# Query up projection in packed tiles, one mean and one square sum per norm, and the norms' factors made on all partitions

## The chip, the core and the metric

The kernel runs on one core of a Trainium2 chip. The metric is the device time of one execution in microseconds (us), as the median of several runs. Times are told with the names of the core's engines: TensorE (PE, its weight loads PEld), VectorE (DVE), ScalarE (ACT), GpSimd (POOL) and SyncE (SP, which issues the DMAs).

## What is computed

One sequence of 512 tokens with 1024 channels goes through two blocks of two layers each; weights and activations are fp32. Cut to what the change touches:

```python
# first block, layer i = 0, 1
y = mixer_ab(x, ...) if i == 0 else mixer_c(x, ...)
x = layer_norm(ALPHA * x + y, ln_mix_g[i], ln_mix_b[i])
f = conv_ffn(x, ...)
x = layer_norm(ALPHA * x + f, ln_ffn_g[i], ln_ffn_b[i])
x = x + sigmoid(x @ ple_w_gate[i]) * (p[i] @ ple_w_proj[i])

# second block, layer l = 0, 1
h = rms_norm(x, norm_g[l])          # then four branches, gates, merge
x = x + acc @ w_out
# at the end
return rms_norm(x, final_norm_g)

# inside mixer_ab: eight heads, 64 channels without and 32 with a rope
cq = rms_norm(h[..., o3:o4], q_norm, RMS_EPS)             # 384 channels
qb = (cq @ w_q_up).reshape(B, S, 8, 64 + 32)
qb = concat([qb[..., :64], apply_rope(qb[..., 64:], cos_b, sin_b, 32)])
ckv = rms_norm(h[..., o4:o5], kv_norm, RMS_EPS)           # 256 channels
```

A layer norm subtracts the mean over the channels, divides by the root of the variance plus 1e-5, and applies a gain and a bias; an RMS norm divides by the root of the mean square plus 1e-6 and applies a gain.

## The kernel before

**Layout.** Activations lie with channels on the 128 partitions and the 512 tokens along the free dimension; x is eight such tiles (slots, named `s`). A weight matrix comes by DMA in 512 KB pieces (`st`), which ACT copies into a rounded high part `h` and DVE into the rest `l`; activations are split likewise. A product of two such operands is three fp32r matmuls (`mm3`: high by high, high by low, low by high). Sums lie in PSUM banks named by their tag: three `d`, two `S`, one `o`, two `m`. Ordinary fp32 operands, which the norms' matmuls have, take two records per matmul in the trace.

**Norms.** A norm over channels needs sums across partitions. Whole projections that end in a norm are done in halves of 256 tokens (`HALVES`); the norm of the first half runs while PE does the second half of the projection, and that of the second half while PE does the first half of what follows (`project`, `group`, `tick`). There are 4 layer norms (8 halves; `Layernorm`) and 3 RMS norms (6 halves; `Rms`: ahead of each layer of the second block, and at the very end), and the two whole-width norms of the latents in `mixer_ab` (`rms`). In a layer norm, `feed` adds up the tiles as they come, in two partial sums on POOL; three matmuls with the constant matrix `meanw` (1/1024 everywhere) sum both and the last tile into a bank, on all partitions. DVE subtracts the mean, ACT squares, DVE and POOL add the squares in two partial sums (`square`). `rstd` makes the factor: one matmul per 128 tokens and partial sum, with the squares as weights and one column of `meanw` moving, puts the sum of each token on a partition; DVE adds epsilon, POOL raises to -0.5; and a matmul with that column as weights, spread over 128, and the identity moving, puts the factor on all partitions again. DVE multiplies (out of PSUM), ACT applies gain and bias (layer norm) and copies the high part, DVE subtracts to get the low part, and PE's next products read both.

**Query up projection.** `prepb(j)` makes the queries of heads 2j and 2j+1: per head one tile of 96 output channels (64 and 32), nine matmuls with 96 weight columns each, a rope over all 96 rows (`rope`: two DVE instructions and two on POOL; the table has 1 and 0 for the first 64 rows), and a split (ACT, DVE).

**The order of the work.** The program is first recorded (`Rec.add`) and then put in order by a planner (`Rec.order`): each engine takes, of the operations that its estimates show as ready, the one with the lowest key; the key is the place in the recording, changed by the table `MOVES` (292 entries of the form first:count, engine, shift). The order of the recording in the first mixer is written out in `ORDER_AB`. All instructions are issued from one line, L680, so the profile shows that line for all of them and groups are told apart by tile names. Activation tables are placed when the program is built: a load stands ahead of a function that the set then loaded does not hold.

Of the kernel before, what the change touches and what calls it, by code (L numbers as in the profile page):

```python
# [13 lines left out]
F32R = mybir.dt.float32r  # L14
# [3 lines left out]
ALU = mybir.AluOpType  # L18
# [59 lines left out]
def _consts():  # L78
# [31 lines left out]
    for i in range(128):  # L110
        r = i % 64
        if r < 16:
            sel[8 + r % 8, 0, i] = 1
            sel[r % 8, 1, i] = -1 if r < 8 else 1
        else:
            sel[64, 0, i] = 1
        if i < 64:
            sel[64, 2, i] = 1
        else:
            r = i % 32  # L120
            sel[32 + r % 16, 2, i] = 1
            sel[16 + r % 16, 3, i] = -1 if r < 16 else 1
# [27 lines left out]
def _layout(i):  # L150
# [14 lines left out]
    a["qup"] = _tiles(i["ab_w_q_up"][0], 6, 96)  # L165
# [95 lines left out]
820:255v-105 1084:103*+49 722:36v-308 1616:34*+52 1965:4*+14 1574:51*+93 1106:7*+62 84:34*+626 1159:22*-127  # L261
446:33*-615 1906:60t-81 505:117*-42 787:69*-425 106:162*+401 1350:14t+359 402:130t-96 1746:61t+219 1011:260t+64
1380:106v+460 455:44*-78 485:18*+14 1162:31*+39 1176:17*-377 357:12*+199 1135:15*-23 878:153v+150 492:14t+120
96:144*-557 1108:293s-272 1022:243t+39 181:3t+644 0:113*+27 1743:5t+166 1168:15*+283 1353:360s-107 1071:22*+71
1904:22t-6 1516:181t+70 1939:14t+72 1100:6t+326 2125:8*-41 1399:10*-553 1807:4t-263 28:268*+13 2076:4*-686
1539:268*-30 1467:52v+164 1150:2*+99 1021:181*-30 1538:41t-149 1235:39v+248 1457:10*+20 1141:185*-5 1496:91*+12
1531:52*+9 1235:13*-270 1172:13t+230 1394:128*-30 1206:5*+87 1745:4*+494 1190:23*-5 2083:3s+246 1321:78t-26
1356:40*-12 1340:33t-505 1313:22*-111 1688:3*-272 1795:17*+172 1117:171*-15 1133:72*+5 1366:97*-9 2113:27t+652
1178:3t+63 1611:2*-399 1211:39v+291 1148:271*+20 1639:52*-116 1111:37*-182 1223:259v+350 1323:88*+59 953:325*+61
1436:33*-22 1137:38*-415 1103:155*-74 1105:7*+610 1474:13t-115 970:219t-128 1115:72*+45 796:392t-38 2073:70*+536  # L270
1077:2t-261 560:47*-252 1165:24t+37 617:6t-333 1668:27t-195 2123:5*+10 2081:210v-9 1181:34*-242 1467:2*-37
1122:21*-213 1138:255t+17 1106:70*+151 4567:114*-71 6914:44*-527 6986:17t-94 6524:388v+762 4439:113*-732 6522:9*-420
# [1940 lines left out]
```

## Time and profile before

| | before |
|---|---|
| median of 3 runs | 2402.99 us (2402.49 to 2403.5) |
| the profiled execution | 2402.8 us |
| its span in the trace | 2401.0 us |
| PE busy | 2378.2 us, 12100 matmul records |
| DVE, ACT, POOL busy | 1433.7, 1017.1, 489.7 us |
| mean granted clock of PE | 0.999 of full speed |
| table loads on ACT | 4 of 1283 ns |

Busy time is the union of an engine's instructions; matmuls overlap in it, so the time that one matmul adds is read from the chain of work that ended last, or from the starts of its neighbours, and not from its mean duration.

### The profile page before, as it was taken

How to read it: one execution, taken by the hardware profiler on the slowest of the kernel's cores; microseconds unless marked ns; L12 is line 12 of the kernel's file. 1: busy time of each engine (PE TensorE's matmuls, PEld its weight loads, DVE VectorE, ACT ScalarE, POOL GpSimd, SP SyncE). 2: the span in 40 equal slices, each digit the busy share in tenths (PEclk: the TensorE clock that was granted, in tenths of full speed). 3: DMA queues.
4: the chain of work that ended last, by engine and by line, in shares of the span. 5: the costliest groups of instructions: out<-in, count | busy, mean ns of one | idle time of the engine just before them, and what ended most of it. 6: DMA issues, size and time to landing. Idle time of an engine off the chain costs nothing.

```text
span 2401.0 us, 31174 instructions
## 1 busy us (share of the span) xinstructions
PE 2378.2 (99%) x12100; PEld 1927.6 (80%) x12100; DVE 1433.7 (60%) x2433; ACT 1017.1 (42%) x1732; POOL 489.7 (20%) x453
## 2 busy tenths in 40 slices
PE   9999999999999999999999999999999999999998
PEld 6766788888888777988888998777788987777887
DVE  5587775354475857664454765667643646686435
ACT  5564463242364646542332554433233334433232
POOL 1332321010131421220110330411222103111221
PEclk9999999999999999999999999999999999999999
DMA  5112222233233113232322252221323432213331
GB/s 191 54 35 73 77 91 97 97 97 97 88 113 100 55 52 97 79 115 97 97 97 97 80 172 88 80 75 49 113 98 117 143 99 78 79 45 104 106 96 62
DMA packets 73513, 220.87 MB, mean 92 GB/s; under 512 B 9557, under 2 KB 13397, under 8 KB 73366
## 3 DMA queue, kind: packets, MB, share of 16 engines
q1 hardware_dynamic: 73366, 218.89, 28.3%
q8 instruction: 95, 1.56, 0.3%
q14 instruction: 52, 0.43, 0.1%
HBM read 210.46 MB, written 8.39 MB: 91 GB/s over the span
## 4 chain that ended last, share of the span: by engine, by line
PE 95%; DVE 2%; ACT 2%; issue 1%; DMA 1%; SPq 0%; POOL 0%; POOLq 0%; DVEq 0%; ACTq 0%
PE d L680 76%; PE S L680 11%; PE m L680 4%; PE o L680 4%; ACT s L680 1%; DVE s L680 1%; DVE sm L680 0%; DVE l L680 0%; DMA s<-in_x 0%; DVE S L680 0%; DMA s<-in_pos 0%; ACT h L680 0%; SPq L680 0%; DVE mt L680 0%; POOL s L680 0%
## 5 line engine op out<-in xcount | busy, mean ns | idle before, releaser
L680 PE MATMUL d<-s,h 128*128 128x512 f32 (+1 forms) x5536 | 1659.8, 380 | 2.8 <-ACT s L680 1.8
L680 PEld LDWEIGHTS d<-s,h 128*128 128x128 f32 x5536 | 1013.7, 188 | 205.9 <-issue 17.5
L680 PE MATMUL d<-s,l 128*128 128x512 f32 (+1 forms) x2768 | 1040.2, 378 | 0.0
L680 DVE TENSOR_TENSOR l<-st,h 128x1024 fp32r<-128x1024 f32 (+3 forms) x379 | 467.0, 1236 | 511.5 <-ACT h L680 504.9
L680 ACT ACTIVATE h<-st 128x1024 fp32r<-128x1024 f32 (+4 forms) x379 | 388.5, 1026 | 815.9 <-PE d L680 656.9
L680 POOL TENSOR_TENSOR s<-s,s 128x512 f32<-128x512 f32 (+3 forms) x319 | 407.0, 1281 | 1118.4 <-DVE s L680 550.1
L680 PEld LDWEIGHTS d<-s,l 128*128 128x128 f32 x2768 | 520.1, 188 | 98.3 <-issue 5.3
L680 ACT ACTIVATE s<-s 128x512 f32<-128x512 f32 (+6 forms) x515 | 270.4, 542 | 356.7 <-DVE s L680 264.9
L680 DVE TENSOR_TENSOR s<-s,s 128x256 fp32r<-128x256 f32 (+6 forms) x337 | 198.7, 603 | 82.9 <-ACT s L680 68.8
L680 PE MATMUL S<-s,s 64*128 64x512 f32 (+10 forms) x752 | 173.0, 378 | 2.7 <-ACT s L680 2.1
L680 PEld LDWEIGHTS S<-s,s 64*128 64x128 f32 (+5 forms) x752 | 103.0, 185 | 63.4 <-ACT s L680 20.8
L680 POOL TENSOR_SCALAR s<-s 128x512 f32<-128x512 f32 x44 | 29.1, 662 | 570.9 <-ACT s L680 570.7
L680 PE MATMUL S<-s,h 128*128 128x256 f32 x704 | 143.5, 285 | 0.1
L680 DVE TENSOR_TENSOR s<-d,s 128x512 f32<-128x512 f32 (+4 forms) x135 | 79.6, 592 | 101.3 <-PE d L680 99.0
L680 DVE SCALAR_TENSOR_TENSOR s<-s,d 128x512 f32<-128x512 f32 x152 | 103.6, 682 | 32.8 <-PE d L680 30.4
L680 DVE SCALAR_TENSOR_TENSOR s<-s,s 128x512 f32<-128x512 f32 (+4 forms) x143 | 100.8, 708 | 37.2 <-ACT s L680 36.1
L680 PEld LDWEIGHTS S<-s,h 128*128 128x128 f32 x704 | 114.4, 191 | 1.3 <-issue 0.8
L680 PE MATMUL S<-s,l 128*128 128x256 f32 x352 | 99.4, 284 | 0.1
L680 ACT ACTIVATE s<-d 128x512 f32<-128x512 f32 (+3 forms) x159 | 89.2, 564 | 22.1 <-PE d L680 21.9
L680 PE MATMUL o<-s,s 128*128 128x128 f32 (+4 forms) x576 | 95.3, 407 | 0.0
L680 ACT ACTIVATE s<-S,sm 128x512 f32<-128x512 f32 x96 | 65.2, 683 | 61.8 <-DVE sm L680 61.8
L680 PE MATMUL d<-h,s 128*128 128x512 f32 (+1 forms) x252 | 79.4, 377 | 5.7 <-ACT s L680 5.7
(148 smaller groups left out, 1455.4 us busy)
## 6 DMA issues: line engine op xcount, KB each, us to landing
st<-in_win SPq DMA_DIRECT2D x112, 512.0 KB, 3.4
st<-in_gu SPq DMA_DIRECT2D x88, 512.0 KB, 3.4
st<-in_dn SPq DMA_DIRECT2D x44, 512.0 KB, 3.4
st<-in_pg SPq DMA_DIRECT2D x16, 512.0 KB, 3.4
st<-in_cqk SPq DMA_DIRECT2D x16, 512.0 KB, 3.4
st<-in_wbr SPq DMA_DIRECT2D x16, 512.0 KB, 3.5
st<-in_wo SPq DMA_DIRECT2D x16, 512.0 KB, 3.5
st<-in_abin SPq DMA_DIRECT2D x14, 512.0 KB, 3.2
```

Source lines behind the costliest of these rows:

```text
L680: getattr(getattr(s.nc, o.eng), o.call)(*[val(v) for v in o.args], **{k: val(v) for k, v in o.kw.items()})
```

## The change

Four edits to the computation, and a new table of moves.

1. The weight of the query up projection is laid out in six tiles of 128 columns instead of eight of 96: the 32 rope channels of four heads in one tile (two such tiles), the 64 other channels of two heads in one (four). `prepb` runs the rope on a tile of four heads once in two calls, splits it, and copies the parts into the heads' slots.
2. A layer norm's `feed` adds all eight tiles into one sum, the last two on DVE; one matmul makes the mean.
3. The two partial sums of squares are added on DVE before PE sums them.
4. `rstd` does one matmul with the constant matrix as weights and the sum of squares moving, 256 columns (512 in `rms`), which gives the mean square on all partitions; the factor is then made there: DVE adds epsilon, ACT does Ln and Exp with a scale of -0.5, and three DVE instructions refine the result (one Newton step). It lies in an SBUF slot, and the multiplications read it from there.
5. `MOVES` has 845 entries.

```diff
-    a["qup"] = _tiles(i["ab_w_q_up"][0], 6, 96)
+    wq = i["ab_w_q_up"][0].reshape(384, 8, 96)
+    rp, np_ = (lambda h: wq[:, h:h + 4, 64:].reshape(384, 128)), (lambda h: wq[:, h:h + 2, :64].reshape(384, 128))
+    a["qup"] = _tiles(np.concatenate([rp(0), np_(0), np_(2), rp(4), np_(4), np_(6)], 1), 6)
...
 MOVES = """
-820:255v-105 1084:103*+49 722:36v-308 1616:34*+52 1965:4*+14 1574:51*+93 1106:7*+62 84:34*+626 1159:22*-127
...
-    def rstd(s, ts, w, eps, c=slice(0, 512), tag="m", ticks=0):
+    def rstd(s, t, w, eps, c=slice(0, 512), tag="m", ticks=0):
         nc = s.nc
-        q0, n = c.start // 128, (c.stop - c.start) // 128
-        pm = s.bank(tag)
-        for q in range(q0, q0 + n):
-            for i, t in enumerate(ts):
-                nc.tensor.matmul(pm[:, q:q + 1], lhsT=t[:, 128 * q:128 * q + 128], rhs=w, start=i == 0,
-                                 stop=i == len(ts) - 1)
-        r = s.small(4)
-        nc.vector.tensor_scalar(r[:, :n], pm[:, q0:q0 + n], eps, None, op0=ALU.add)
-        s.pow_(r[:, :n], r[:, :n])
+        pm, r, u = s.bank(tag), s.slot(), s.slot()
+        p, q, v = pm[:, c], r[:, c], u[:, c]
+        nc.tensor.matmul(p, lhsT=w, rhs=t[:, c], start=True, stop=True)
         yield ticks
-        pb = s.bank(tag)
-        for q in range(n):
-            o = c.start + 128 * q
-            nc.tensor.matmul(pb[:, o:o + 128], lhsT=r[:, q:q + 1].to_broadcast([128, 128]), rhs=s.ident, start=True,
-                             stop=True)
-        return pb
+        nc.vector.tensor_scalar(v, p, eps, None, op0=ALU.add)
+        nc.scalar.activation(q, v, AF.Ln)
+        nc.scalar.activation(q, q, AF.Exp, scale=-0.5)
+        nc.vector.scalar_tensor_tensor(v, v, -0.5, q, op0=ALU.mult, op1=ALU.mult)
+        nc.vector.tensor_mul(v, v, q)
+        nc.vector.scalar_tensor_tensor(q, v, 1.5, q, op0=ALU.add, op1=ALU.mult)
+        s.free(u)
+        return r
...
+            nc.vector.tensor_add(ts[0][:, c], ts[0][:, c], ts[1][:, c])
+            pb = yield from s.rstd(ts[0], s.meanw, RMS_EPS, c, "mo"[i], 2)
...
-            if j % 4 == 0:
-                t[i, j // 4] = s.slot()
-            elif j % 4 == 1:
-                s.pool_add(t[i, j // 4][:, c], X[j - 1][:, c], X[j][:, c])
-            elif j != 7:
-                s.pool_add(t[i, j // 4][:, c], t[i, j // 4][:, c], X[j][:, c])
+            if j == 0:
+                t[i] = s.slot()
+            elif j == 1:
+                s.pool_add(t[i][:, c], X[0][:, c], X[1][:, c])
+            elif j < 6:
+                s.pool_add(t[i][:, c], t[i][:, c], X[j][:, c])
+            else:
+                s.nc.vector.tensor_add(t[i][:, c], t[i][:, c], X[j][:, c])
...
-            for k, t in enumerate((t0, t1, X[7])):
-                nc.tensor.matmul(pm[:, c], lhsT=s.meanw, rhs=t[:, c], start=k == 0, stop=k == 2)
+            nc.tensor.matmul(pm[:, c], lhsT=s.meanw, rhs=n.t[i][:, c], start=True, stop=True)
...
-            pb = yield from s.rstd(acc, s.meanw[:, :1], LN_EPS, c, tag, 2)
+            nc.vector.tensor_add(acc[0][:, c], acc[0][:, c], acc[1][:, c])
+            pb = yield from s.rstd(acc[0], s.meanw, LN_EPS, c, tag, 2)
...
-        s.meanq = mk("meanq", [128, 1], 1.0 / 384)
-        s.meank = mk("meank", [128, 1], 1.0 / 256)
+        s.meanq = mk("meanq", [128, 128], 1.0 / 384)
+        s.meank = mk("meank", [128, 128], 1.0 / 256)
...
+            if j % 2 == 0:
+                rq = s.rope(s.dense("qup", (0, 3)[j // 2], L["cq"]), CB, SB, ROT16)
+                L["rq"] = s.split(rq)
+                s.free(rq)
+            yield
+            pq = s.dense("qup", (1, 2, 4, 5)[j], L["cq"])
             for e in range(2):
-                rq = s.rope(s.dense("qup", 2 * j + e, L["cq"], m=96), CB, SB, ROT16, 96)
-                QB[j, e] = s.split(rq, 96)
-                s.free(rq)
-                yield
+                qh, ql = QB[j, e] = s.slot(F32R), s.slot(F32R)
+                r, o = slice(64 * e, 64 * e + 64), 32 * (2 * j % 4 + e)
+                nc.scalar.activation(qh[:64], pq[r], AF.Copy)
+                nc.vector.tensor_sub(ql[:64], pq[r], qh[:64])
+                nc.vector.tensor_copy(qh[64:96], L["rq"][0][o:o + 32])
+                nc.scalar.activation(ql[64:96], L["rq"][1][o:o + 32], AF.Copy)
```

How the instructions stand is read from the built programs. First ACT, in the second half of the layer norm behind the mixer of layer 1. Before, the squares (`s_8985`, `s_8992`) are followed by a weight copy (`h`), an evacuation (`s<-d`) and the gain and bias of the first tile:

```order
L680 ACTIVATE s_8985<-s_7911 128x256
L680 ACTIVATE s_8992<-s_7920 128x256
L680 ACTIVATE h_8997<-st_8759 128x1024
L680 ACTIVATE s_9009<-d_8874 128x512
L680 ACTIVATE s_7847<-s_7847,c_cols 128x256
L680 ACTIVATE s_8889<-s_7847 128x256
```

In the change, at the same place (`s_8978` is the factor; the first instruction on it is Ln, the second Exp):

```order
L744 ACTIVATE s_8937<-s_7849 128x256
L744 ACTIVATE s_8956<-d_8819 128x512
L744 ACT_TABLE_LOAD
L744 ACTIVATE s_8978<-s_8970 128x256
L744 ACT_TABLE_LOAD
L744 ACTIVATE s_8978<-s_8978 128x256
L744 ACTIVATE s_7794<-s_7794,c_cols 128x256
L744 ACTIVATE s_8757<-s_7794 128x256
```

Four instructions have come in, two of them loads of activation tables. The same pattern stands in 12 of the 14 halves; only the first layer norm has Ln and Exp without loads. The built program has 28 table loads where that of before has 4.

Then PE at the same norm. Before (`o_9007` takes the sums, `o_9039` is the broadcast):

```order
L680 MATMUL o_9007<-meanw,s_8843 128x1
L680 MATMUL d_8899<-s_8943,l_8826 128x256
L680 MATMUL o_9007<-meanw,s_8848 128x1
L680 MATMUL o_9007<-meanw,s_8843 128x1
L680 MATMUL o_9007<-meanw,s_8848 128x1
...
L680 MATMUL S_9031<-s_8915,h_8997 128x256
L680 MATMUL o_9039<-identr,sm_9021 128x128 x2
L680 MATMUL S_9031<-s_8925,h_8997 128x256
...
L680 MATMUL S_9031<-s_8981,l_9012 128x256
L680 MATMUL d_8895<-s_8889,h_8720 128x256
```

In the change (`o_8965` is the one product; `s_8757` is the first tile of the normalized half, which the last two rows read):

```order
L744 MATMUL S_8830<-s_8813,l_8788 128x256
L744 MATMUL o_8965<-s_8895,meanw 128x256
L744 MATMUL S_8830<-s_8826,h_8734 128x256
...
L744 MATMUL S_8885<-s_8837,h_8871 128x256
L744 MATMUL S_8885<-s_8861,h_8871 128x256
L744 MATMUL S_8885<-s_8837,l_8961 128x256
L744 MATMUL S_8885<-s_8757,h_8871 128x256
L744 MATMUL S_8830<-s_8757,h_8734 128x256
```

The four sums and two broadcasts are one product, and 28 products of 256 columns stand between it and the first that reads a normalized tile; before, 33 of them and the broadcast stand between the last sum and the first reader (`s_8889`).

## Rows read from the trace of the kernel before

**Rows 1.** The page: engines' busy time, and the chain's shares by engine.

```profile
PE 2378.2 (99%) x12100; PEld 1927.6 (80%) x12100; DVE 1433.7 (60%) x2433; ACT 1017.1 (42%) x1732; POOL 489.7 (20%) x453
...
PE 95%; DVE 2%; ACT 2%; issue 1%; DMA 1%; SPq 0%; POOL 0%; POOLq 0%; DVEq 0%; ACTq 0%
```

**Rows 2.** The chain in order of time (start us, us, engine and tile, count).

```profile
330.64 316.62 PE d L680 x1401
```

**Rows 3.** The chain from 676 to 705 us: its longest piece.

```profile
683.20 3.62 ACT s L680 x11
```

**Rows 4.** The chain at norms: latents, a mean, ordinary products, sums, a broadcast.

```profile
123.71 2.77 PE m L680 x24
...
130.49 0.89 PE m L680 x8
...
660.59 1.30 PE m L680 x6
661.88 1.42 PE d L680 x12
...
1894.17 0.79 PE m L680 x8
...
1897.93 0.44 PE m L680 x4
```

**Rows 5.** Groups by form: out<-in, shapes, count | busy us, mean ns | idle before.

```profile
L680 PE MATMUL d<-s,h 128*96 128x512 f32 x48 | 16.4, 408 | 0.5 <-DVE s L680 0.5
...
L680 PE MATMUL d<-s,l 128*96 128x512 f32 x24 | 9.6, 401 | 0.0
...
L680 PE MATMUL o<-meanw,s 128*128 128x1 f32 x56 | 7.4, 233 | 1.3 <-DVE s L680 1.3
...
L680 PE MATMUL m<-s,meanw 128*128 128x256 f32 x24 | 6.4, 387 | 0.0
...
L680 PE MATMUL o<-identr,sm 128*128 128x128 f32 x28 | 4.3, 277 | 1.0 <-POOL sm L680 1.0
```

**Rows 6.** Timeline of the end: start us, us, instruction [idle before <-releaser].

```profile
2391.18 0.42 DVE L680 TENSOR_TENSOR s<-s,s 128x256 f32<-128x256 f32 x1 [0.48 <-ACT s L680]
...
2391.66 0.83 PE L680 MATMUL o<-meanw,s 128*128 128x1 f32 x6 [1.31 <-DVE s L680]
...
2394.28 3.22 DVE L680 SCALAR_TENSOR_TENSOR s<-s,c_cols,o 128x256 f32<-128x256 f32 x8 [1.59 <-PE o L680]
```

**Rows 7.** Timeline of a layer norm's second half behind layer 1's mixer.

```profile
1003.14 0.72 PE L680 MATMUL o<-meanw,s 128*128 128x1 f32 x6
...
1005.72 0.60 PE L680 MATMUL o<-identr,sm 128*128 128x128 f32 x4
...
1006.36 1.74 DVE L680 TENSOR_TENSOR s<-s,o 128x256 f32<-128x256 f32 x5 [2.03 <-PE o L680]
...
1006.82 0.60 ACT L680 ACTIVATE s<-s,c_cols 128x256 f32<-128x256 f32 x1 [3.33 <-DVE s L680]
...
1007.46 0.42 ACT L680 ACTIVATE s<-s 128x256 fp32r<-128x256 f32 x1
...
1008.20 0.28 PE L680 MATMUL d<-s,h 128*128 128x256 f32 x1
```

**Rows 8.** Groups by form: DVE's three-operand instruction on 256 columns.

```profile
L680 DVE SCALAR_TENSOR_TENSOR s<-s,s 128x256 f32<-128x256 f32 x24 | 12.8, 551 | 4.3 <-ACT s L680 4.1
```

**Rows 9.** Timeline of ACT around two table loads.

```profile
18.09 1.06 ACT L680 ACTIVATE h<-st 128x1024 fp32r<-128x1024 f32 x1 [1.27 <-DMA st<-in_abv]
19.17 1.28 ACT L680 ACT_TABLE_LOAD   x1
24.51 0.63 ACT L680 ACTIVATE s<-s 64x512 f32<-64x512 f32 x1 [4.06 <-DVE s L680]
25.16 1.28 ACT L680 ACT_TABLE_LOAD   x1
26.46 1.06 ACT L680 ACTIVATE h<-st 128x1024 fp32r<-128x1024 f32 x1
```

More of the change, by code (lines that the diff above doesn't have):

```diff
@@ L116, in _consts @@
             sel[64, 0, i] = 1
[L117 to L122, printed above, removed]
+        r = i % 32
+        sel[32 + r % 16, 2, i] = 1
+        sel[16 + r % 16, 3, i] = -1 if r < 16 else 1
     c["ropesel"] = sel.reshape(65, 512)
@@ L266 @@
[L266 to L270, printed above, removed]
@@ new lines @@
+11349:59*+414 10437:150*+2 9279:139*-41 13227:36*+13 13254:9t+1 11259:10*+4 11517:154*+58 11216:244*+479
+13046:74*-18 13069:29*+12 13060:6*+66 9303:24*-11 11616:128*-14 11394:11*-68 10575:14*-92 11509:106*+18
+11931:365*-15 11699:14*+21 11771:27*-252 11999:317*+277 11486:8s+349 10590:6t+5 11557:2*+241 11513:291*+8
+12001:156*-24 12078:10*+95 11529:326*+13 11429:10t-309 11750:188t+12 9327:3*+677 11263:251*+60 11544:216s+251
+10490:2*-659 10620:116s+82 12805:63*-330 11743:5*-384 9296:31*-14 11425:108s+660 11707:40*-14 10365:372s-198
@@ new lines @@
+14359:62*+11 15300:2*+7 14277:20*-188 14256:78*-39 14497:64*+18 14039:101*-74 15290:42*+387 14718:171t-459
+14672:54t+27 15099:3*+293 13979:353*+5 13018:61v+62 14318:20t-750 14313:15*-37 15288:44*+442 13003:90*+34
+15149:57*+378 15149:50*-536 14954:4*-778 15044:10*+415 15125:89t-676 15123:3t+763 13062:42v+29 15298:40*+649
+15158:155*-447 15196:295t+258 15268:64*+53 15140:311t-527 13150:90*-224 13794:14*-118 1415:384*-4 1982:310*-257
+1001:264*-23 1288:137t-8 908:49s+368 1212:170t-80 1207:6t+535 1039:138v+210 1365:16*+96 1349:7t-478 1266:15*-107
@@ new lines @@
+1309:11*-200 1440:41*-2 1788:4t+392 1647:2*+168 1393:291t+6 1743:101*-144 1209:16*-143 1036:14*-76 795:8*-57
+1743:6*+191 1237:7*+85 1617:35*-60 1157:13*-399 1674:41*+16 1117:197v-338 1183:32*-139 662:326*-6 1344:189v-338
+985:17*-8 1048:14s-403 1935:7*+54 1933:3*+106 1215:5*-255 1604:7t-463 1186:6t-330 1143:99*-757 1625:75*-42
+1747:69*-109 1288:34*+91 61:12*+107 1770:77*-71 1786:6*-112 1210:17*+28 1745:42*+181 52:113*+19 56:16t+65
+1197:70*+26 1772:45*-293 1214:4*-604 1401:2*-186 1238:9*+59 2080:5*-460 1759:35*+244 2070:171*-4 1786:220*+185
@@ L965, in rms @@
             s.square(acc, j, x, c)
-        r = s.rstd(acc, w, RMS_EPS)
+        nc.vector.tensor_add(acc[0], acc[0], acc[1])
+        r = s.rstd(acc[0], w, RMS_EPS)
         next(r)
@@ L977, in rms @@
             s.free(y)
+        s.free(pb)
         return out
@@ L996, in half @@
                 s.out.extend((s.slot(F32R), s.slot(F32R)) for _ in range(8))
-            pb = yield from s.rstd(n.acc[i], s.meanw[:, :1], RMS_EPS, c, "mo"[i], 2)
-            s.free(*n.acc[i])
+            ts = n.acc[i]
+            nc.vector.tensor_add(ts[0][:, c], ts[0][:, c], ts[1][:, c])
+            pb = yield from s.rstd(ts[0], s.meanw, RMS_EPS, c, "mo"[i], 2)
+            s.free(*ts)
             for j, x in enumerate(s.x):
```

121 lines of the change are left out of this document (90 added, 31 removed).

## Prediction

> **What bounds the kernel now.** I read the page first. TensorE (PE) is busy for 99% of the span, and the chain that ended last lies on it for 95% [rows 1]. A busy PE need not be a PE at its peak, so I went on to the chain: over 1401 products of 512 columns in a row it needs 316.62 us, 0.226 us each, without a piece of another engine between [rows 2]. PE's stream of instructions is therefore the bound: what leaves it shortens the run, and what makes it wait lengthens it. DVE (60%), ACT (42%) and POOL (20%) have room on the whole, so their work counts only where PE waits for it. That is at the norms, where a product needs a tile that DVE and ACT are still scaling. There the chain does leave PE: in the norm behind the first FFN it stays 3.62 us on ACT in one piece [rows 3].
>
> The profiled execution took 2402.8 us: its span of 2401.0 and 1.8 around it. The sum is made against that; the median of the three runs, 2402.99, is 0.2 above it.
>
> **What leaves PE.** The prices are those of the chain, which charges a group with the time by which it pushes the end of PE's stream.
>
> Sums of squares: per half of 256 tokens eight records for the sums cost 0.79 us and four for the broadcast 0.44, so 1.23 [rows 4]. The records are two per fp32 product: 56 for the sums in one bank and 28 for the broadcasts are seven halves, and the other bank has the other seven [rows 5]. In their place comes one fp32 product of 256 columns. Three of those, the mean of a half, cost 1.30, so one costs 0.43 [rows 4]. Saved: 1.23 - 0.43 = 0.80 in each of 14 halves, 11.2 us.
>
> Means: one of three products stays in each of the 8 layernorm halves: 0.87 x 8 = 7.0 us.
>
> The norms of the query and key latents: 32 records cost 2.77 + 0.89 us, 0.114 each [rows 4]; both norms have 48 (32 of sums, 16 of broadcasts), 5.5 us. Two products of 512 columns remain, at twice 0.43: 1.7. Saved 3.8 us.
>
> Query up projection: 48 + 24 = 72 products with 96 weight columns [rows 5] become 54 with 128. Eighteen fewer at 0.226 are 4.1 us. A product with 128 weight columns is what the 0.226 was read from.
>
> Together 11.2 + 7.0 + 3.8 + 4.1 = **26.1 us**; I allow 24 to 29, since a single fp32 product between others may cost 0.1 more than a third of three, and the 96-column products may have cost more than 0.226 when they changed the shape of the array.
>
> **What is added, and what hides it.** In the projections the ropes on DVE and POOL shrink from eight to two, and ACT and DVE get four short copies for each head pair; PE has other tiles' products there, so I count nothing, and 2 us either way if that cover is gone. Two of the adds of a layernorm's mean move from POOL to DVE, and each norm gets one more DVE add of its two partial sums; they lie ahead of the new product, in the same chain, 0.42 us each [rows 6].
>
> The large item is the factor's chain. Before, DVE's add, POOL's power and PE's broadcast took from 1003.14 to 1006.36, 3.2 us, from the last sums to the first scaling [rows 7]. Now it is: product 0.43 and the read behind it 0.28 (from the broadcast's start at 1005.72, plus its 0.36 up to the next product, to 1006.36 [rows 7], with 0.44 for the broadcast in the chain [rows 4]); DVE's add from PSUM 0.42; Ln 0.42; Exp 0.42; three dependent DVE instructions, between 0.42 and 0.55 each [rows 7, 8], together 1.45; hops 0.15. That is 3.6 us where Ln and Exp follow each other. But the built program sets a table load between them, and one ahead of Ln, in 12 of the 14 halves: 28 loads instead of 4, because tanh's set does not hold Ln and the set then loaded for Ln does not hold Exp. A load takes 1.28 us [rows 9]. The one ahead of Ln can run while Ln's input is still being made: the load at 19.17 ran while the instruction behind it waited for DVE until 24.51 [rows 9]. The one between Ln and Exp can't hide: Exp needs Ln's result. So the chain is 3.6 + 1.3 = 4.9 us, 1.7 above before, and 6.2 if the first load is late too.
>
> The Trainium skill (ScalarE: Activation LUTs, What ACT_TABLE_LOAD costs) speaks against the change: each switch costs some 1283 ns of load and 1380 ns of drain, 2.66 us. By that, the chain would be 1.4 us longer for each load on it. The trace agrees on the load (1.28) and shows no drain: the load at 25.16 begins 0.02 us behind the end of the function before it, and the next instruction starts at 26.46, 0.02 behind it [rows 9].
>
> From the scaling to PE's first reader it is 1.84 us for a layernorm (1006.36 to 1008.20, over ACT's 0.60 and 0.42 [rows 7]) and about 1.25 for an RMS norm, which lacks the first ACT step. So a half needs, from its sums' product to the first reader, about 6.5 us in a layernorm with loads, 5.2 in the first layernorm, which has none, and 5.9 in an RMS norm.
>
> Against that stands what PE has to do in between. I counted the rows of the changed order from that product to the first reader of the scaled tiles, at 0.226 for 512 columns, 0.12 for 256 (1.42 for 12 [rows 4]) and 0.43 for the fp32 product. In the order of the program, first and second half: 6.7 and 3.9 (first layernorm, mixer of layer 0), 8.2 and 5.8 (its FFN), 9.0 and 3.6 (mixer of layer 1), 6.5 and 5.0 (its FFN), 6.3 and 3.5 (first RMS norm), 4.5 and 5.3 (second). Two groups need a remark: at 8.2 four ACT rows stand between Exp and the first tile and the first reader wants the third tile, so some 1.4 us are missing; at 4.5 the first reader wants the second tile, 1.5. The others miss what the difference says: 1.1, 0.5, 2.7, 1.3, 2.2 and 0.4 (with 0.2 given to each cover for the slower start behind an fp32 product). Sum 11.1 us. The first table load may be late by up to 1.28 in the four halves where ACT has weight copies and evacuations to do just ahead of it, 0 to 5; some 2 us of waits that stand at these places today go. I take **10 us**, ends 1 (the covers hold, since the sums' product can also come earlier than its inputs are waited for now) and 20.
>
> The end of the program has no cover: last partial sum at 2391.18 + 0.42, scaling at 2394.28, 2.7 us [rows 6]. Now an add 0.45, then 4.9: 5.3. **2.6 us** more, 3.9 if the first load shows as well.
>
> **The table of moves** is replaced as a whole, so instructions stand in another order everywhere. PE changes between array shapes about as often as before (by the order), and PE's time outside the norms is already product behind product [rows 2]. I count 0, ends -4 and +4.
>
> Sum: 2402.8 - 26.1 + 10 + 2.6 = 2389.3; **2389 us**.
>
> **The rivals.** (1) *The covers hold.* PE finds other products wherever the chains grew, and only the end of the program pays: 2402.8 - 26.1 + 1 + 2.6 = 2380. For it: in the norms of today PE mostly has such work. Against: second halves of 3.5 to 3.9 us of cover for chains of 5 to 6.5.
>
> (2) *A switch costs twice its row*, because the pipe runs empty first. Ten halves with readers and the end pay 1.28 more each: 2389 + 14 = 2403, no change. By the Trainium skill's drain (the same page and section) it would be 15 for these 14; that is the rule, and the trace of before does not agree with it. Against it stand the gaps of 0.02 us around the loads [rows 9].
>
> (3) *ACT takes PE's place at the norms*, slower than before. ACT works in order: while Ln waits for DVE, and during two loads, neither PSUM banks nor weights get through it. If each chain waits for both loads and for two weight copies of 1.06 us [rows 9], the six layernorm halves with loads need 9.9 us and the four RMS halves 9.3, 97 against covers of 58: 2402.8 - 26.1 + 39 + 3.9 = 2420. It decides from 24 us of waits on, 2.4 per half. For it: the 3.62 us of ACT in the chain [rows 3]. Against: ACT has 58% idle, and the weight copies can stand elsewhere.
>
> (4) *The order gives the gain back elsewhere*: new waits of PE in the projections or attention of some 8 us: 2397.
>
> **How the numbers follow.** Chances: forecast 0.53, (1) 0.26, (2) 0.06, (3) 0.05, (4) 0.10. The range of 8 in 10 takes in the forecast with its bounds and most of (1) and (4): 2376 to 2399. Within 0.2% (about what a measurement of this kernel can tell from no change: 2398.2 to 2407.8) lie (2) and some of (4): 0.09. Slower by over 0.2%: 0.05. Faster: 0.86.
>
> **What would show it.** Right: PE's instructions down by some 230 records, PE still at 98 to 99%, 28 table loads of about 1.28 us, the factor's chain near 5 us with PE waiting 1 to 3 us ahead of second halves, the last scaling 2.6 us later behind the last partial sum. Wrong: no such waits (rival 1), a gap of over a microsecond beside each load (rival 2), PE's share at 97% or less with ACT's part of the chain grown to several per cent (rival 3), or long waits of PE away from the norms (rival 4).

## The result: slower by 0.8%

The changed kernel took **2422.1 us** (median of 4 runs, 2420.8 to 2423.8) against 2403.1 for the kernel before on the same chip: a ratio of 1.008, 95% interval 1.0062 to 1.0097. The forecast was 2389, in 2376 to 2399. The profiled execution has a span of 2421.7 us, 20.7 above that of before. On the chip that ran no_loads, one_load and the two plain runs below, the kernel before fell into two groups, near 2403 and near 2407.5 us, so a difference to its median there, 2405.8, is uncertain by 2 to 3 us.

The page of the changed kernel: busy time by engine, and the chain by engine.

```profile
PE 2369.3 (98%) x11866; PEld 1908.7 (79%) x11866; DVE 1461.2 (60%) x2504; ACT 1069.9 (44%) x1797; POOL 452.6 (19%) x425
...
PE 35%; DVE 2%; ACT 1%; issue 0%; POOL 0%; DVEq 0%; ACTq 0%
```

PE has 234 records less than in [rows 1], as forecast, and yet the span is longer. DVE gained 27.5 us of work and ACT 52.8. The chain can't be read here: its shares add up to 38%. Followed back from the end it stops at 1476.79 us, at a small product of the second block. The added table loads are not the reason, since the run without them (no_loads) has a chain of 39%. So I went to the waits of PE (engine and tile, who was waited for: us in total, times, longest us). Of the kernel before the first row reads:

```profile
PE d L680 <- ACT s L680: 7.5, 3, 5.7
```

Of the changed kernel:

```profile
PE d L744 <- ACT s L744: 22.5, 13, 6.0
PE d L744 <- DVE s L744: 5.8, 6, 3.0
PE S L744 <- ACT s L744: 5.0, 4, 2.5
PE o L744 <- DVE s L744: 2.1, 2, 2.0
```

The 5.7 and 6.0 are the start of the program; nearly all the rest of these rows is at the norms and the end, and most of it is PE waiting for ACT.

**Where the 20.7 us are.** I took the starts of all PE records and gave each record a price: the median time to the next record of its form in the kernel before (the mean, where a form's times alternate). The sum of the prices is PE's *work*; what the records took above their prices are *waits*, with the time that a slow clock costs among them. The rest is the time up to PE's first record and behind the start of its last.

| us of the profiled execution | up to the first | work | waits | behind the last | span |
|---|---|---|---|---|---|
| before | 5.7 | 2334.9 | 53.3 | 7.1 | 2401.0 |
| changed | 6.0 | 2307.4 | 97.2 | 11.1 | 2421.7 |
| difference | +0.3 | **-27.5** | **+43.9** | +4.0 | +20.7 |

So what the prediction took off PE did leave PE, and more than that came back as waits. By place, waits alone (the norms with what their first readers wait for):

| waits, us | mixer 0 | norm behind mixer 0 | behind FFN 0 | behind mixer 1 | behind FFN 1 | first RMS | second RMS | end |
|---|---|---|---|---|---|---|---|---|
| before | 10.5 | 1.1 | 3.4 | 1.8 | 0.9 | 0.2 | 0.4 | 2.7 |
| changed | 13.0 | 4.1 | 7.9 | 11.8 | 11.3 | 6.9 | 6.0 | 4.4 |

The longest is in the norm behind layer 1's mixer. ACT's timeline there (start us, us, instruction, count [idle before <-releaser]), then PE's:

```profile
977.96 1.28 ACT L744 ACT_TABLE_LOAD   x1
979.25 0.42 ACT L744 ACTIVATE s<-s 128x256 f32<-128x256 f32 x1
979.68 1.28 ACT L744 ACT_TABLE_LOAD   x1
980.98 0.42 ACT L744 ACTIVATE s<-s 128x256 f32<-128x256 f32 x1
981.30 1.04 ACT L744 ACTIVATE h<-st 128x1024 fp32r<-128x1024 f32 x1
...
986.10 0.58 ACT L744 ACTIVATE s<-d 128x512 f32<-128x512 f32 x1
```

```profile
982.77 0.39 PE L744 MATMUL d<-s,l 128*128 128x512 f32 x1
986.73 1.22 PE L744 MATMUL d<-s,h 128*128 128x512 f32 x2 [3.57 <-ACT s L744]
```

Load, Ln, load, Exp stand without a gap: both loads are in line. PE doesn't wait for a scaled tile here. It waits for the evacuation of a PSUM bank (`s<-d`, from 986.10 for 0.58 us), which stands in ACT's queue behind the two loads, a weight copy and the first scalings.

And the wait costs twice. The same stretch in windows of 2.5 us (busy us of PE, PEld, DVE, ACT, POOL with counts, granted clock of PE, DMA share, GB/s):

```profile
982.50:985.00 2.50, 0.66 (x3) 0.19 (x1) 2.46 (x8) 1.67 (x4) 0.00 (x0) 1.00 0.11 44
985.00:987.50 2.50, 0.77 (x2) 0.68 (x3) 2.50 (x7) 2.44 (x6) 0.37 (x1) 0.52 0.00 0
987.50:990.00 2.50, 2.50 (x8) 1.92 (x7) 2.50 (x6) 2.43 (x6) 2.34 (x3) 0.50 0.32 88
...
992.50:995.00 2.50, 2.50 (x20) 2.37 (x19) 1.02 (x3) 2.00 (x3) 0.00 (x0) 1.00 0.00 0
```

PE stood still from 983 to 986.7, and the granted clock fell from 1.00 to 0.50, from 2.4 to 1.2 GHz; three products took 1.28 us (988.18 to 989.46) where 0.68 is their price. Five such stretches, 20.5 us in all, lie at the norms of the changed kernel, and none at those of the kernel before; the records in them took 8.4 us above their prices.

### The profile page after: what moved, and what is told of

It reads as the page before. It is cut to its first block, busy times and chain, and to the rows that moved or that the text cites. A ratio compares the mean times of both kernels' runs of the same rounds, so it can differ in the third digit from the quotient of the medians.

```text
span 2421.7 us, 30774 instructions
## 1 busy us (share of the span) xinstructions
PE 2369.3 (98%) x11866; PEld 1908.7 (79%) x11866; DVE 1461.2 (60%) x2504; ACT 1069.9 (44%) x1797; POOL 452.6 (19%) x425
## 5 line engine op out<-in xcount | busy, mean ns | idle before, releaser
L744 DVE TENSOR_TENSOR l<-st,h 128x1024 fp32r<-128x1024 f32 (+3 forms) x378 | 460.3, 1220 | 524.8 <-ACT h L744 516.6
L744 ACT ACTIVATE h<-st 128x1024 fp32r<-128x1024 f32 (+3 forms) x378 | 387.9, 1028 | 775.5 <-PE d L744 670.7
L744 POOL TENSOR_TENSOR s<-s,s 128x512 f32<-128x512 f32 (+2 forms) x307 | 384.5, 1258 | 1214.1 <-DVE s L744 625.3
L744 ACT ACTIVATE s<-s 128x256 f32<-128x256 f32 (+6 forms) x549 | 286.1, 536 | 368.2 <-DVE s L744 269.1
L744 DVE TENSOR_TENSOR s<-s,s 128x256 f32<-128x256 f32 (+5 forms) x443 | 232.2, 552 | 85.8 <-ACT s L744 71.0
L744 PE MATMUL S<-s,s 64*128 64x512 f32 (+12 forms) x752 | 172.0, 378 | 2.2 <-DVE mt L744 1.7
L744 DVE SCALAR_TENSOR_TENSOR s<-s,s 128x512 f32<-128x512 f32 (+4 forms) x175 | 118.5, 680 | 62.6 <-ACT s L744 61.0
L744 PEld LDWEIGHTS S<-s,s 64*128 64x128 f32 (+5 forms) x752 | 102.4, 185 | 63.7 <-ACT s L744 20.8
L744 DVE TENSOR_TENSOR s<-d,s 128x512 f32<-128x512 f32 (+2 forms) x137 | 80.9, 594 | 91.7 <-PE d L744 87.7
L744 ACT ACTIVATE s<-d 128x512 f32<-128x512 f32 (+3 forms) x167 | 94.3, 566 | 21.6 <-PE d L744 20.5
```

The costliest lines, as they stand in the source:

```text
L744: getattr(getattr(s.nc, o.eng), o.call)(*[val(v) for v in o.args], **{k: val(v) for k, v in o.kw.items()})
```

## The experiments

Each run stands beside the kernel before on the same chip. "Difference" is median less median.

| run | median us | before there | ratio (95%) | difference |
|---|---|---|---|---|
| changed | 2422.1 | 2403.1 | 1.008 (1.0062 to 1.0097) | +19.0 |
| no_loads | 2401.3 | 2405.8 | 0.9984 (0.9975 to 0.9994) | -4.5 |
| one_load | 2411.3 | 2405.8 | 1.0021 (1.0011 to 1.0030) | +5.5 |
| before_plain | 2446.3 | 2405.8 | 1.0173 (1.0156 to 1.0189) | +40.5 |
| after_plain | 2462.2 | 2405.8 | 1.0242 (1.0224 to 1.0259) | +56.4 |
| no_chain | 2392.0 | 2403.0 | 0.9955 (0.9940 to 0.9970) | -11.0 |
| dve_chain | 2409.2 | 2403.0 | 1.0023 (1.0013 to 1.0032) | +6.2 |
| pool_pow | 3133.0 | 2403.0 | 1.3041 (1.3020 to 1.3063) | +730 |
| less_pe | 2396.9 | 2403.0 | 0.9975 (0.9965 to 0.9985) | -6.1 |
| less_dve | 2403.0 | 2403.6 | 0.9999 (0.9990 to 1.0008) | -0.6 |
| less_both | 2396.1 | 2403.6 | 0.9968 (0.9957 to 0.9980) | -7.5 |
| no_chain_pe | 2409.6 | 2403.5 | 1.0025 (1.0015 to 1.0035) | +6.1 |
| old_factor | 2390.2 | 2403.5 | 0.9946 (0.9933 to 0.9958) | -13.3 |
| aware_order | 2403.5 | 2403.1 | 1.0001 (0.9991 to 1.0011) | +0.4 |
| short_chain | 2386.2 | 2403.1 | 0.9928 (0.9913 to 0.9943) | -16.9 |

In most of them the order of the program they start from was kept: the planner saw that program, and only when its instructions were issued did others take their places or were left out. That matters here, since the table of moves fits one program only. The edits are shown in short: what is issued, not every line of the kernel.

### Is it the loads? no_loads, one_load

```diff
 # no_loads: issued in the places of Ln and Exp
-        nc.scalar.activation(q, v, AF.Ln)
-        nc.scalar.activation(q, q, AF.Exp, scale=-0.5)
+        nc.scalar.activation(q, v, AF.Copy, scale=0.0)
+        nc.scalar.activation(q, q, AF.Copy, scale=1.0, bias=rho)
 # one_load: ahead of Ln
+        nc.scalar.preload_act_table_set("natural_log_exp_and_others")
```

Expected of no_loads:

> The changed kernel in its own order, with one thing taken out: Ln and Exp of the factor are replaced by two copies of the same size on ACT (a constant start value takes the place of Ln's and Exp's result, so the factor is only approximate), and with them the 24 added table loads go; 4 loads stay. Everything else, the number of instructions on each engine included, is as in the changed kernel. Theory A (the loads carry the loss: they stand in ACT's queue ahead of the factor and of what PE waits for): each of the 12 halves with loads gets 1.3 to 2.6 us shorter, so some 16 to 31 us of the waits go, half of the 8 us at half clock behind them, and 2.6 of the tail: 2380 to 2400 us. Theory B (the loads are hidden, the longer chain of dependent instructions and the order of the work make the waits): less than 8 us go, 2414 us or more.

Expected of one_load:

> The changed kernel in its own order, computing the same: ahead of each Ln stands an explicit load of the table set that holds both Ln and Exp, so no load stands between the two any more; 27 loads instead of 28, because the two halves of the first layernorm now have one too. Theory A with both loads on the path: one load less, 1.28 us, in each of 12 halves, 15 us, and some of the half clock: 2400 to 2408 us. Theory A with only the first load on the path (ACT comes late to it) or theory B: within 5 us of the changed kernel, 2417 to 2424.

Theory A held, at its lower end: the time, 2401.3, is 1.3 above its range, but 20.3 us of waits went, of the 16 to 31 expected. Without the 24 loads the kernel goes from +19.0 to -4.5, so the **loads cost 23.5 us** beside each chip's base; the times as they stand differ by 20.8 and the spans by 21.3. That is 0.9 to 1 us a load. With one of the two in each half gone, 13.5 come back beside each base, 10.8 time against time; 2411.3 lies between the two cases that one_load was to decide. The place shown above, ACT and PE with one load:

```profile
977.50 1.28 ACT L746 ACT_TABLE_LOAD   x1
978.80 0.87 ACT L746 ACTIVATE s<-s 128x256 f32<-128x256 f32 x2
...
985.01 1.06 PE L746 MATMUL d<-s,h 128*128 128x512 f32 x2 [2.29 <-ACT s L746]
```

and PE without loads:

```profile
983.33 0.73 PE L746 MATMUL d<-s,h 128*128 128x512 f32 x2 [1.55 <-ACT s L746]
```

3.57, 2.29, 1.55: the load between Ln and Exp is there with its whole 1.28 us, the one ahead of Ln with 0.74, as part of it ran while Ln's input was still made. In the norm behind FFN 1 ACT's evacuation holds PE for 2.4, 1.2 and 0 us in the same three runs, in the second half of the first RMS norm a scaled tile does for 2.7, 1.5 and 0. Seen over the program, no_loads has 20.3 us of waits less than the changed kernel (76.9 against 97.2): 14.4 of them long waits of PE at the norms, 1.8 at the end, and 4.2 half clock that went with the waits.

The Trainium skill (ScalarE: Activation LUTs, Table sets: the hidden batching unit) says that Ln and then Exp need one load, since one set holds both. The built program took two in each half, because Ln was given a set without Exp; where that set was loaded by an instruction of the kernel, as in one_load, the trace shows the rule, and it was worth 10.8 to 13.5 us.

### Is it the order? before_plain, after_plain

Both kernels with `MOVES = ""`.

> The kernel before with its table of moves emptied, so that the planner alone sets the order. It has no reading alone; it is the base for the changed kernel without its table. The planner itself puts the end 32 us later without the table: 2420 to 2450 us.

> The changed kernel with its table of moves emptied. Theory C (the replaced order is at fault: its moves put too little work between the factor and its readers): without either table the changed kernel is 10 to 26 us faster than the kernel before without its table. Theories A and B (the cause is in the factor's chain, whatever the order): it is slower by 10 to 30 us, as with the tables.

Theory C fell. Without tables the changed kernel is slower by 16.0 us, with them by 19.0. The tables are worth 40 and 37 us, but the loss doesn't come from having replaced one by the other.

### The rest of the chain: no_chain, dve_chain, pool_pow

```diff
 # no_chain, issued: the factor is a constant; Ln, Exp and two DVE instructions left out
-        nc.vector.tensor_scalar(v, p, eps, None, op0=ALU.add)
+        nc.vector.tensor_scalar(v, p, 0.0, rho, op0=ALU.mult, op1=ALU.add)
...
-        nc.vector.scalar_tensor_tensor(q, v, 1.5, q, op0=ALU.add, op1=ALU.mult)
+        nc.vector.tensor_copy(q, v)
 # dve_chain, issued in the places of Ln and Exp
+        nc.vector.scalar_tensor_tensor(q, v, 0.0, v, op0=ALU.mult, op1=ALU.mult)
+        nc.vector.tensor_scalar(q, q, rho, None, op0=ALU.add)
 # pool_pow, issued in the place of Ln; the four instructions behind it become one copy
+        nc.gpsimd.tensor_tensor(v, v, m, op=ALU.pow)
```

> The changed kernel in its own order without the factor's chain: Ln, Exp and two of the three DVE instructions behind them are left out and a constant stands for the factor (so the norms are only approximate); DVE's read of the product and one DVE copy stay. PE's program is as in the changed kernel. Against the run without loads (2401 us) ACT loses 28 instructions and the chain gets some 2 us shorter. If the length of the chain makes the waits that are left (1.4 to 3.1 us at eight places): 2 us less at each of them and at the end, 2383 to 2390 us. If they come from the order and from other steps of the norm: 2395 us or more.

> As the run without loads, but the two instructions in Ln's and Exp's place run on DVE instead of ACT, 0.42 us each as there (the factor is approximate as in that run). The chain has the same steps and nearly the same length; only ACT's queue no longer has an instruction that waits for DVE, with weight copies and evacuations behind it. If ACT's order makes the waits that are left: 2390 to 2396 us. If the chain's length does: 2399 to 2404, as without loads.

> The changed kernel in its own order, computing the same: the power -0.5 of all partitions and columns by one POOL instruction in place of Ln, Exp and the first two DVE instructions behind them, a DVE copy in place of the third; no added loads. The power of 128x4 took 1.02 us. If that is mostly a fixed price, 128x256 takes 1 to 2 us and the kernel 2383 to 2396 us. If it goes by the element (0.26 us a column), 65 us in each of 14 halves with cover for some 5: over 3000 us.

no_chain lies between its two cases: 6.5 us below no_loads beside each base (-11.0 against -4.5), 9.3 time against time. So the steps of the chain beyond the loads cost 6.5 to 9.3, and some 16 of PE's 27.5 us are still missing with no chain at all. dve_chain came out against both of its theories: it is *slower* than no_loads, by 10.7 us beside each base, by 7.9 time against time and by 4.5 in the spans, although only two instructions of 0.42 us moved from ACT to DVE in each half; DVE is busy for 10.8 us more (1473.5 against 1462.7). So taking the two out of ACT's queue wins nothing on the whole, and work added to DVE costs at least four tenths of its time here. Where this arises is known only in part: in the profiled execution PE has a new wait of 1.8 us for DVE ahead of the query latents' product. pool_pow was expected to show whether POOL's power goes by the element, and it does: 128x256 took 41.5 us and 128x512 82.4, 0.16 us a column. Both forms together:

```profile
L746 POOL TENSOR_TENSOR s<-s,mhalf 128x256 f32<-128x256 f32 (+1 forms) x16 | 745.5, 46596 | 59.8 <-DVE s L746 59.8
```

So the power on all partitions is no way out, and the columns of the kernel before, 128x2 in 0.85 us, are the cheap form of it.

What holds PE in no_chain? The norm behind FFN 1 has the longest wait, DVE first, then PE, then the window of 8 us (as above):

```profile
1353.18 2.06 DVE L746 TENSOR_TENSOR s<-s,o 128x256 f32<-128x256 f32 x6
1355.17 1.09 DVE L746 TENSOR_TENSOR s<-s,s 128x256 f32<-128x256 f32 x3
1356.17 0.74 DVE L746 TENSOR_TENSOR s<-s,o 128x256 f32<-128x256 f32 x2
1356.84 2.43 DVE L746 TENSOR_TENSOR s<-s,s 128x256 f32<-128x256 f32 x7
```

```profile
1358.31 0.39 PE L746 MATMUL d<-s,h 128*128 128x256 f32 x1 [2.94 <-DVE s L746]
```

```profile
1352.00:1360.00 8.00, 4.61 (x27) 3.84 (x26) 7.35 (x23) 7.94 (x21) 2.59 (x3) 0.93 0.23 74
```

PE wants the low part of a scaled tile. DVE makes it at 1357.84, the fourth instruction of the last row, behind eight subtractions of the mean for the other half (`s<-s,o`) and six other instructions (`s<-s,s`). DVE is busy for 7.35 of these 8 us and ACT for 7.94, while PE is for 4.61. Here PE is not the bound. The kernel before has no such wait in this norm, so it came with the change; which of the edits brought it, no run tells.

### Does PE's saving come through? less_pe, less_dve, less_both, no_chain_pe

```diff
 # less_pe: the kernel before, with one product a mean for three, one a sum for two
-            for k, t in enumerate((t0, t1, X[7])):
+            for k, t in ((2, X[7]),):
...
-            for i, t in enumerate(ts):
+            for i, t in ((1, ts[1]),):
 # less_dve: the kernel before, with every second subtraction of the mean left out
-                nc.vector.tensor_sub(x[:, c], x[:, c], pm[:, c])
+                if j % 2 == 0: nc.vector.tensor_sub(x[:, c], x[:, c], pm[:, c])
 # no_chain_pe: no_chain, with the mean's and the factor's product issued three times each
```

> The kernel before in its own order, with 52 fp32 products of PE left out and nothing else: two of the three mean products in each of 8 halves (the mean is then made from the last partial sum alone), and half of the sums of squares (one of the two partial sums is left out). By the prices of the prediction: 16 x 0.43 = 7.0, 28 x 0.2 = 5.5 and 8 x 0.22 = 1.8, 14.3 us: 2389 us. If PE's products around the norms lie beside other waits, so that a saving there isn't the end's: 2396 us or more.

> The kernel before in its own order with 32 DVE instructions left out and nothing else: in each layernorm half four of the eight subtractions of the mean (128x256, 0.42 us each, 13.4 us of DVE in all; those four tiles keep their mean). PE's program is whole. Theory P (PE is the bound at the norms): PE waits there for 5 us at most today, so 0 to 3 us go, 2400 to 2403. Theory V (the vector side is as full as PE at the norms, and each holds the other): likewise little, 0 to 5 us, since PE's products stay; this run is the other corner of the pair with less_both.

> The kernel before in its own order with both cuts: the 52 fp32 products of less_pe left out (14.7 us of PE, which gave 6 us), and the 32 DVE instructions of less_dve. Theory V: the 8 us that less_pe lost came back as waits for DVE's work at the norms, and with 13.4 us less of that they go: 2386 to 2390 us, more than the two cuts give one by one. Theory P' (the 8 us were lost to something else, the order of PE's stream or evacuations by ACT): 2393 to 2397, as less_pe with at most what less_dve gives.

> The run without the factor's chain (2392 us) in the same order, with PE work put back: each layernorm half makes its mean product three times, each of the 14 half norms its product for the sum of squares three times (the same product into the same bank), 44 fp32 products more, 44 x 0.43 = 18.9 us of PE. That is about what the change took from PE at the norms. If what leaves PE at the norms shortens the run one for one, as the prediction summed it: 2411 us. If PE's freed time there became waits, as in less_pe (6 of 14.7 us came through): about 8 us, 2396 to 2403.

less_pe takes only the prediction's sums and means off PE, in the order that the kernel before was given. PE's work fell by 13.7 us (2321.2 against 2334.9; 14.3 were summed), and the time by 6.1. I followed the gain through the program, PE record by record against the kernel before: at each first half of a layer norm 0.7 to 1.2 us are won and 0.65 to 0.7 lost again within 2 to 8 us. These four places make some 2.7 of the 7.6 us that did not come through; the rest went in smaller pieces. One such place behind FFN 0, DVE, then PE:

```profile
664.20 1.21 DVE L682 TENSOR_TENSOR l<-st,h 128x1024 fp32r<-128x1024 f32 x1
665.33 0.41 DVE L682 TENSOR_TENSOR s<-d,s 128x256 f32<-128x256 f32 x1
```

```profile
665.89 0.70 PE L682 MATMUL d<-s,h 128*128 128x512 f32 x2 [0.54 <-DVE s L682]
```

PE came earlier to a product whose PSUM bank DVE had still to empty, behind the split of a weight piece. My theory V, that DVE's load at the norms takes the gain, made two tests: less_dve did nothing, as both theories expected, but less_both gave 7.5 where 13 to 17 were expected of V (2396.1 us, in the 2393 to 2397 of its rival). V fell. At the same place in less_both

```profile
664.98 1.23 DVE L682 TENSOR_TENSOR l<-st,h 128x1024 fp32r<-128x1024 f32 x1 [0.19 <-ACT h L682]
...
666.69 0.70 PE L682 MATMUL d<-s,h 128*128 128x512 f32 x2 [0.33 <-DVE s L682]
```

DVE would be free in time, but now its split waits for ACT's copy of the same piece, and PE's wait for DVE is 0.2 us shorter, not gone. At this place it is not one engine's load; in the norm behind FFN 1 the wait is gone in less_both. My reading of it: in an order searched until PE hardly waits, the three queues are set to one another, and an engine that gets faster meets the next one.

no_chain_pe is the opposite test, and went against what I expected from less_pe: 44 products put back (15.6 us of work by the prices) cost 17.6. So PE's work still counts in the changed kernel's order; *adding* to PE cost all of it there, *taking away* gave half in the order of before. Both are what a path looks like where several engines are near the end of their room.

### A better order, a shorter chain: aware_order, short_chain, old_factor

```diff
 # aware_order: in the planner, where ACT's functions switch; the set with both is loaded ahead of Ln
+                elif str(f) in s.SETS and cur not in s.SETS[str(f)]:
+                    t = max(t, free[e] + 1283)
...
 # short_chain: one instruction makes the (constant) factor, and the order is searched for that
+        nc.vector.tensor_scalar(q, p, 0.0, rho, op0=ALU.mult, op1=ALU.add)
 # old_factor: one tile of squares, sums as columns, power and broadcast as in the kernel before
+            nc.tensor.matmul(pm[:, q:q + 1], lhsT=t[:, 128 * q:128 * q + 128], rhs=w[:, :1], start=True, stop=True)
```

> The changed kernel, computing the same, with two things added: the order is searched anew by a planner that counts a table load of 1283 ns wherever ACT's functions switch, and where Ln finds another set loaded, the set that holds Ln and Exp is loaded ahead of it; 19 loads in place of 28. If the loss of the changed kernel comes from loads that its order was not made for, that an order can put where ACT is free: 2395 to 2402 us, no slower than the kernel before. If a chain of six steps over ACT and DVE can't be covered at the norms by any order of this program: 2406 us or more.

> The changed kernel with the factor's chain left out (one DVE instruction writes a constant factor behind the product, so the norms are approximate), as in no_chain, but with an order searched for that program. no_chain, in the changed kernel's order, had 2392 us: 18 above 2403 - 29, what PE's smaller work alone would give. If those 18 are waits that the order holds because it was made for the long chain: 2376 to 2385 us. If they are the price of the other edits (adds on DVE, the single mean, the packed query) in any order: 2389 to 2393.

> Computes the same. The changed kernel's packed query projection, single mean product and single tile of squares, but the factor as in the kernel before: sums as columns, now of one tile instead of two (half the products), DVE's add, POOL's power of 128x2, PE's broadcast; no Ln, no Exp, no added loads. The table of moves is searched anew for this program. By the prediction's prices PE loses 5.5 (half of 14 x 0.79) + 7.0 (means) + 4.1 (query) + 1.8 (latents) = 18.4 us. If an order made for the program turns most of that into time: 2384 to 2391 us. If less than half of what leaves PE at the norms comes through, whatever the order: 2393 to 2397.

Each of the three has a table searched for it, with 2902 entries in aware_order, 2198 in short_chain and 4937 in old_factor, against 845 in the changed kernel and 292 before. So part of what they gain may come from the longer search itself; the changed kernel's own order was not searched further, and this rival stays open in all three.

aware_order has 19 loads, eight of them set by the kernel and eleven by the compiler (line, engine, count | busy us, mean ns | idle before):

```profile
L1023 ACT ACT_TABLE_LOAD x11 | 14.1, 1283 | 0.9 <-PEq L2562 0.7
L1022 ACT ACT_TABLE_LOAD x8 | 10.3, 1283 | 0.1
```

and comes back to the kernel before, +0.4 us, a shade above the 2402 of its better case. The loads' 21 to 23.5 us can mostly be bought back by another order and 9 loads fewer, but no more than that.

short_chain gives 5.9 us over no_chain, by its own order and by one DVE copy less in each half; its 2386.2 lies between its two cases. So of the 16 us that no_chain lacked, up to 6 belonged to an order made for the long chain; 10.6 are left in this order too. Of those, some 4 are waits up to and in the norm behind mixer 0, and 5.1 in the norm behind FFN 1 (6.0 against 0.9).

old_factor computes the same as both kernels and is **faster than both: 2390.2 us**, within the 2384 to 2391 expected if most of the saving comes through; 13.3 below the kernel before, 31.9 below the changed one.

```profile
PE 2363.8 (99%) x11978; PEld 1912.5 (80%) x11978; DVE 1428.6 (60%) x2456; ACT 1017.8 (43%) x1741; POOL 467.6 (20%) x441
```

It keeps the packed query, the single mean and the single square tile, 18.1 us of PE's work (2316.8 against 2334.9; 18.4 were summed), and has the chain and the 4 loads of the kernel before; DVE (1428.6 us) and ACT (1017.8) have no more work than there [rows 1]. Waits of PE:

```profile
PE d L1263 <- ACT s L1263: 6.5, 2, 6.1
PE o L1263 <- DVE s L1263: 3.4, 4, 2.0
PE o L1263 <- POOL sm L1263: 1.4, 2, 1.0
```

Beyond the start and the end hardly one is left. The kernel before was not searched further either, so how the 13.3 us split between the edits and the order stays open.

### The sum

| step | from | to | us |
|---|---|---|---|
| work taken off PE, if all of it came through | before | | -27.5 |
| the loads | no_loads | changed | +23.5 |
| two ACT steps, two DVE steps | no_chain | no_loads | +6.5 |
| an order made for the long chain, one DVE copy a half | short_chain | no_chain | +5.9 |
| left with a short chain in its own order | -27.5 | short_chain | +10.6 |
| the change | before | changed | +19.0 |

The rows add up because each is the difference of two neighbours. The border between the loads and the other steps is the least sure: 23.5 and 6.5 beside each chip's base, 20.8 and 9.3 time against time, 21.3 and 11.0 in the spans. The loads are the largest item by each.

## Why the prediction was wrong, point by point

**What leaves PE: right.** 26.1 us were summed, 24 to 29 allowed; the records' prices give 27.5, and the count was met (234 records).

**That all of it shortens the run: wrong, and in the first lines.** "What leaves it shortens the run" was read from 99% busy and a chain that is PE [rows 1, 2]. That says that PE hardly waits in this order. It doesn't say that nothing else is as late. less_pe measured what PE's time at the norms is worth in the order of before: 6.1 of 13.7 us. In an order searched for the program, old_factor, 13.3 of 18.1 came through.

**What hides the factor's chain: the step that failed.** The waits at the norms were put at 10 us, 20 at most. They grew by 40.2: 31.8 by PE's waiting, 8.4 by the clock. Of the longer single waits, those in second halves came out as forecast: 8.2 in sum, and waits of 0.7 to 2.7 measured, 9.8 in all. The *first* halves did not: 2.9 forecast, 19.5 measured. There I had counted the rows from the product to the first reader of a scaled tile and found cover of 6.3 to 9.0 us, 4.5 in the second RMS norm. But PE doesn't need only the scaled tiles. Among those covering products are some whose PSUM bank ACT must empty, and ACT stood in Ln, Exp and two loads; that is the wait of 3.57 us above. And the first reader is not the last: behind FFN 1 the low part of a later tile came some 3 us late, behind DVE's work for the other half, with a chain or without one. I had named ACT's order of work as a rival and as a bound of 1.28 us in four halves; I hadn't listed what stands behind Ln in ACT's queue and who waits for that. There is a slip in the sum too: 4.9 + 1.84 are 6.7 and not 6.5, and likewise 5.4 and 6.2 stand for 5.2 and 5.9; with eight waits counted that is some 2 us, which does not matter beside the 30 that were missing.

**The loads.** Their number (28) and time (1283 ns) were right, and so was the prediction's doubt of a drain: 979.67 to 979.68 us is all that lies between Ln and the next load. That the first load would mostly run ahead of its need was wrong: in 8 of 12 halves load, Ln, load, Exp stand in one line, and from the product to the first scaling it took 4.7 to 7.8 us, 5.8 on average, where 4.9 was taken. The load between Ln and Exp was priced as fully in the chain, and the place shown above bears that out (1.28 us).

**The clock.** Nothing in the prediction priced a wait above its own length. The granted clock fell to 1.2 GHz behind five of the waits of 1.3 us and more, and that added 8.4 us to 31.8, a quarter. Behind the others at the norms it did not.

**The end: right in its step.** From the last partial sum to the last scaling it takes 5.3 us, as summed. The rows:

```profile
2410.27 0.70 PE L744 MATMUL o<-s,meanw 128*128 128x256 f32 x2 [1.95 <-DVE s L744]
```

```profile
2411.90 1.28 ACT L744 ACT_TABLE_LOAD   x1
2413.20 0.42 ACT L744 ACTIVATE s<-s 128x256 f32<-128x256 f32 x1
```

```profile
2415.02 1.28 DVE L744 SCALAR_TENSOR_TENSOR s<-s,c_cols,s 128x256 f32<-128x256 f32 x3
```

The half ahead of it waits for 1.7 us more than before, which was not summed.

**The projections: 0 forecast, 2 either way; 2.5 measured.** That is more than half of what the packed query saves (4.1). What makes it is not shown. The copies that replace the wide rope are not enough to explain it: old_factor has the same ones, and there PE reaches the first layer norm's mean product at 280.79 us, 2.9 earlier than before (283.69) and 0.3 later than in the changed kernel (280.49), which by the prices saves 2 us more at the latents.

**The rivals.** (3) had the time, 2420, and the mechanism in its main part, ACT standing in PE's way at the norms; it got 0.05, since ACT is idle for 58%. That average was the wrong reason: from 980 to 990 us of the changed kernel, around the longest wait, ACT was busy for 8.9 of 10 us. Of its own signs one did not come, PE's share at 97% or less (it is 98%), and the other, ACT's share of the chain, could not be read. Not every part of it held: no weight copy stands between Ln and Exp, and dve_chain shows that merely taking two instructions of that size off ACT and giving them to DVE wins nothing. That its sum meets the time is partly luck, since a fifth of the 40.2 us is the clock, which it did not count. (2), a switch at twice its row, is excluded by the rows. (4), new waits away from the norms, is at most the 2.5 us of mixer 0. The signs of the forecast nearly all came (234 records less, PE at 98%, 28 loads, waits ahead of second halves, the end): they looked where the prediction had looked, and none of them at a first half.

## What to carry to other kernels

Before a step is moved to an engine that works through its queue in order, as ACT does in the rows above, list what stands behind it in that queue and who waits for each of these, not only who waits for the step's own result; and read that engine's busy share in the stretch, not in the whole. A tuned order in which PE hardly waits is a balance of several queues. Here work added to PE counted in full (17.6 us for 15.6) and work added to DVE in part (4.5 to 10.7 for 10.8); work taken off PE counted by half (6.1 for 13.7) and work taken off DVE counted for nothing that can be told from no change (0.6 for 8.2 of its busy time). So a change is worth a new search of the order before it is judged. Functions of ACT that follow each other belong in one table set, and the trace shows whether they got one.

## What was not expected of the hardware

- After waits of PE of some microseconds the products behind them ran at half speed: granted clock 0.50 to 0.52 from 985.0 to 990.0 us, 1.2 in place of 2.4 GHz, behind a stand of 3.6 us. Behind a shorter wait in the same place (1.55 us in no_loads) they ran at full speed, and so they did in the changed kernel itself behind a wait of 2.57 us that ended at 1440.76. So the length of a wait alone does not tell it.
- POOL's power takes time by the column: 82.4 us for 128x512, 41.5 for 128x256, against 1.02 for 128x4 and 0.85 for 128x2.
- A table load on ACT began 0.02 us behind the instruction before it, and the next one, where its input was there, 0.01 us behind the load: 28 loads of 1.28 us, and no time beside them.
